# A transformer-like layer on one core: the merge projection opens with two jobs in seven products, first loads go out on ScalarE's queue, and the planner's rule for waiting changes

## The chip, the cores and the metric

The kernel runs on one core of one Trainium2 chip. The metric is the device time of one execution in microseconds (us), as the median of the runs. The core has five engines that run side by side and wait for each other through semaphores: TensorE (PE, matrix products into banks of PSUM), VectorE (DVE), ScalarE (ACT), GpSimd (POOL) and SyncE (SP, which here issues most of the DMAs). PEld is the loading of a matmul's stationary operand, which runs beside the matmuls.

## The reference: what is computed

One layer of a hybrid encoder over a sequence of 1024 positions with 1024 channels, in float32:

```python
h = rms_norm(x, norm1_w[l])
proj = h @ w_in[l]                    # q, k, v, gates, x_lru, y_lru: 8192 columns
...
y_a = (o * silu(g_ret)) @ w_ret_o[l]  # branch A: chunkwise retention, group norm
...
y_b = (hl * gelu(y_lru)) @ w_lru_o[l] # branch B: conv, gated linear recurrence
mix = (sigmoid(gate_ret + merge_gate_b[l, 0]) * y_a
       + sigmoid(gate_lru + merge_gate_b[l, 1]) * y_b)
x = x + mix @ w_out[l]                # the merge projection
h = rms_norm(x, norm2_w[l])
up = h @ ffn_w_up[l]                  # 6144 columns
...
x = x + (gelu(gate) * val) @ ffn_w_down[l]
return rms_norm(x, norm_f_w)
```

## The kernel before

**Matrix products.** Every large product is cut into jobs. A job multiplies a stationary block A of 256 rows or columns by 1024 with an operand B of 1024 by 1024. A is cut in 2 x 2 blocks (A11, A12, A21, A22; the second digit is the half of the inner dimension), B in 2 x 2 sets (B11 to B22), each set four tiles of 128 x 512 (j = 0 to 3). Float32 precision comes from a split: each tile is written as hi + lo, with hi a cast on ScalarE (L469) and lo a subtraction on DVE (L470). One product of a block with a set is then 4 tiles x 3 passes (`PASSES`, L399: hi hi, hi lo, lo hi) = 12 matmuls of 128 x 128 by 128 x 512 into one bank.

There are two ways through a job. The plain one, `mm_by` (L660, its matmuls at L680), takes eight products. The fast one, `mm_fast` (L698, matmuls at L718), takes seven, by the scheme of Strassen and Winograd. It needs sums of A's blocks (S1 to S4, formed on DVE in `prep_fast`, L545, at L555 to L564) and sums of B's sets (T1 to T4), and more additions behind the products: ScalarE copies a bank away at L767, and DVE adds at L735 to L771. The order of the seven products is a tuple (L400 to L405): `PRODS`, `ENDING`, `EARLY`, and `FIRST = ("A11", "S3", "A12", "S1", "S2", "A22", "S4")`, which no job uses. When S3 comes before S2 (`back3`, L703), two more DVE additions run, at L769 and L771. A job with `mate=True` is taken together with the next one: each product is done for both before the following one, so that a set of B is read twice in a row. Banks are six (`psg`, L439), tiles for A's blocks 22 (`NW`), all other tiles 81 (`NU`).

**Merge projection.** The four jobs `wjobs` (L1746) compute x + mix @ w_out, 256 positions each. A comes from `mix_d` in DRAM, where the last projection of branch B (`emit_lru_o`, L1396) writes the mixed channels; blocks with inner half 1 can be read when the first four channel groups of 128 are there, those with inner half 2 when all are. B is w_out: `w_out_set` (L1736) loads its sets, and their sums T1 to T4 were formed earlier and lie in `tw_d`. `out_start` (L1742) queues the building of B: the four plain sets first, then the four sums. Job 0 is plain, with inner half 1 ahead of half 2 (`by="k"`), and gives the set B12 back after it (`drop12`); jobs 1 to 3 are fast, one at a time, in the order `PRODS`. `emit_out` (L1667) adds x where the fast path has not (L1673), stores the row block and squares it on ScalarE for the norm that follows.

**What sets the order.** The program is built twice. The first build gives the list of instructions and their dependencies to the class `Plan` (L200). `latest` (L261) goes backwards and finds for each instruction when it is due; `forward` (L307) then lays out every engine in time with the durations of its cost model and takes the instruction with the earliest due time (`rank`) among those that are ready. This holds for the DMAs of SP's queue too, which are held back to what the model lets the DMA engines move. The second build is chained into these orders. At L341 to L346 DVE and ScalarE may be left idle for an instruction that is not ready yet: when it becomes ready within the next one's duration plus `NEAR` (500 ns), is overdue already, and the next one can spare more than `APART` (10,000 ns).

**Start.** The layer begins with the value projection (`values`, L1411). POOL issues the first eight columns of the parameters (L1478), ScalarE's queue the first x tile (L1479), and SP's queue weights and the other x tiles in turn (L1480 to L1491). Twelve matmuls on zeros (L1484) warm TensorE up. The first scaled x tile (L1439, on DVE) needs the parameters and the x tile, and the first matmul (L1454) needs that.

**End.** The last half tile is finished in two pieces by `final_half` (L1886): a sum of squares (L1892), its addition (L1893), a product with the norm's weights (L1894), then the root on POOL (L1897), two scalings (L1902, L1904) and two stores (L1905).

Of the kernel before, what the change touches and what calls it, by code (L numbers as in the profile page):

```python
# [199 lines left out]
class Plan:  # L200
# [5 lines left out]
    READ, WRITE, MOVE, QUEUE = 1900.0, 1500.0, 700.0 / 262144, 500.0  # L206
    LATE_DMA, LATE_PE, BACKLOG, KEEP = 1500.0, 400.0, 300.0, 2000.0
    SURE_DMA = 700.0
    NEAR, APART = 500.0, 10000.0

    @staticmethod
    def read(nc):
# [94 lines left out]
    def forward(self, rank):  # L307

        todo = {n: len(b) for n, b in self.before.items()}
        at = dict.fromkeys(self.steps, 0.0)  # L310
        free = dict.fromkeys(self.ENGINES, 0.0)
        wait = {e: [] for e in self.ENGINES}
        ready = {e: [] for e in self.ENGINES}
        order = {e: [] for e in self.ENGINES}
        moved, table, begin = 0.0, None, []
        for n, k in todo.items():
            if not k:
                heapq.heappush(wait[self.steps[n].eng], (0.0, n))

        def switch(n):  # L320
            f = self.steps[n].func
            return f in self.TABLES and table not in self.TABLES[f]

        left = len(self.steps)
        while left:
            t, e = math.inf, None
            for k in self.ENGINES:
                if not ready[k] and not wait[k]:
                    continue
                when = free[k] if ready[k] else max(free[k], wait[k][0][0])  # L330
                if k == "SP":
                    when = max(when, moved - self.READ - self.BACKLOG)
                if when < t:
                    t, e = when, k
            while wait[e] and wait[e][0][0] <= t:
                n = heapq.heappop(wait[e])[1]
                heapq.heappush(ready[e], (rank[n], n))
            item = ready[e][0]
            if e == "Activation" and switch(item[1]) and item[0] > t + self.KEEP:
                item = min((q for q in ready[e] if not switch(q[1])), default=item)  # L340
            if e in ("DVE", "Activation"):  # L341
                soon = min(((rank[n], at) for at, n in wait[e] if at < t + self.steps[item[1]].hold + self.NEAR),
                           default=None)
                if soon and soon[0] < min(t, item[0] - self.APART):
                    free[e] = soon[1]
                    continue  # L346
            ready[e].remove(item)
            heapq.heapify(ready[e])
            n = item[1]
            s = self.steps[n]  # L350
            if e == "Activation" and switch(n):
                t += self.SWITCH
                table = self.TABLES[s.func][0]
            order[e].append(n)
            if e == "PE":
                begin.append(t)
            left -= 1
            free[e] = t + s.hold
            if s.dma:
                if e == "Pool":  # L360
                    moved += s.bytes * self.MOVE
                    done = t + s.hold + self.landing(s)
                elif s.bytes > 4096:
                    moved = max(t + s.hold + self.landing(s) - s.bytes * self.MOVE - self.QUEUE,
                                moved) + s.bytes * self.MOVE
                    done = moved + self.QUEUE
                else:
                    done = t + s.hold + self.landing(s)
            else:
                done = t + s.hold + s.tail  # L370
            for m in self.after[n]:
                lag = self.lag(s, self.steps[m])
                if lag is not None:
                    if s.dma:
                        lag = max(self.HAND + self.SURE_DMA, min(lag, rank[m] - done))
                    at[m] = max(at[m], done + lag)
                todo[m] -= 1
                if not todo[m]:
                    heapq.heappush(wait[self.steps[m].eng], (at[m], m))
        return order, begin  # L380
# [45 lines left out]
def tile_trunk_layer(ctx, tc, x, xt, positions, params, consts, normf, w_in, w_v, w_ro, w_lo,  # L426
                     w_out, w_up, w_dn, w_gate, out):
    nc = tc.nc
# [895 lines left out]
    def operand(op, fetch, sums=True, sets=("B11", "B12", "B21", "B22")):  # L1324

        keys = [(n, j) for n in sets for j in range(4)]
        for key, (tick, t) in zip(keys, reads(fetch, keys, AHEAD_B)):
            yield from landed(tick)
            op[key] = split(t)
            put(t, late=SOONER)  # L1330
            yield 0.6
        if sums:
            yield from tsets(op, fetch)

    def kept_sums(op, src):

        def fetch(n, j):
            t = get()
            SY.dma_start(t, src[int(n[1]) - 1, j])
            return t  # L1340

        keys = [(f"T{i}", j) for i in (1, 2, 3, 4) for j in range(4)]
        for key, (tick, t) in zip(keys, reads(fetch, keys, AHEAD_B)):
            yield from landed(tick)
            op[key] = split(t)
            put(t, late=SOONER)
            yield 0.6
# [63 lines left out]
    def values():  # L1411
# [10 lines left out]
        def wload(nm, j):  # L1422
            m, kh = int(nm[1]) - 1, int(nm[2]) - 1
            t = raw[nm, j] = vget()
            SY.dma_start(t, w_v[4 * kh + j, :, TH * m:TH * m + TH])

        def xload(nm, j, q=SY):
            kh, h = int(nm[1]) - 1, int(nm[2]) - 1
            t = xs[nm, j] = get()
            q.dma_start(t, xt[4 * kh + j, :, TH * h:TH * h + TH])  # L1430
# [44 lines left out]
                         t.rearrange("p (m c) -> p m c", m=2))  # L1475
            put(t)

        G.dma_start(par[:, 0:8], params[:, 0:8])  # L1478
        xload("B11", 0, nc.scalar)  # L1479
        wload("A11", 0)  # L1480
        S.activation(st[:, 0:1], st[:, 1:2], AF.Sqrt)
        warm = psa.get()
# [2 lines left out]
        psa.put(warm)  # L1485
        for j in (1, 2, 3):
            wload("A11", j)
            xload("B11", j)
        for j in range(4):
            wload("A12", j)  # L1490
            xload("B21", j)  # L1491
# [175 lines left out]
    def emit_out(t, fast):  # L1667
        def emit(m, c, src, unit):
            if fast and unit is not None:
                acc = unit  # L1670
            else:
                acc = wjobs[t].take(m, c)
                V.tensor_add(acc, src, acc)  # L1673
                if unit is not None:
                    put(unit)
            i = 2 * t + m
            ST.dma_start(x1_d[x_row(t, m, c)], acc)
            j = psa.get()
            S.activation(j, acc, AF.Square, accum_out=nst[:, c, i:i + 1])
            psa.put(j)  # L1680
            if t == 3:
                last4[m, c] = acc
            else:
                put(acc)
        return emit

    def out_post(t):
        def fn():
            a, b, v, r, w = (nst[:, i, 2 * t:2 * t + 2] for i in range(5))
            V.tensor_add(v, a, b)  # L1690
            V.tensor_scalar(v, v, 1.0 / D, EPS, ALU.mult, ALU.add)
            G.tensor_tensor(r, v, half[:, 0:2], ALU.pow)
            if t >= 2:
                return norm_half(t - 2)
        return fn
# [44 lines left out]
        return t  # L1740

    def out_start():  # L1742
        builders.append(operand(wop, w_out_set, False))
        builders.append(kept_sums(wop, tw_d))

    wjobs = [Job(lambda m, kh, t=t: mix_d[t, m, kh].rearrange("p k c -> p (k c)"), wop,  # L1746
                 emit_out(t, t > 0), out_post(t), fast=t > 0, last=t == 3, drop12=t == 0,
                 pre=((0, 0), (0, 1), (1, 1)), fetch=from_x(t), by=None if t else "k",
                 order=None if t else ("A11", "A21", "A12", "A22"),
                 ready=lambda m, kh, t=t: all((4 * kh + j, t // 2) in mixed for j in range(4)))  # L1750
             for t in range(4)]
    ojobs[-2].post = out_start
# [86 lines left out]
    nf = []  # L1839
# [46 lines left out]
    def final_half(u, s):  # L1886

        one, two, r = nst[:, 0, 2:3], nst[:, 4, 0:1], nst[:, 3, 2:3]
        if s.start == 0:
            fin["o"], fin["j"] = get(), get()  # L1890
        o, j = fin["o"], fin["j"]
        V.scalar_tensor_tensor(j[:, s], u[:, s], 1.0 / D, u[:, s], ALU.mult, ALU.mult, accum_out=two)  # L1892
        V.tensor_add(one, one, two)  # L1893
        V.tensor_mul(o[:, s], u[:, s], nf[1][:, s])  # L1894
        if s.start == 0:
            return
        G.tensor_tensor(r, one, half[:, 0:1], ALU.pow)  # L1897
        put(u, j)
        for c in range(2):
            t = fin.pop((0, 0)) if c == 0 else o  # L1900
            if c:
                V.tensor_scalar(t, t, r, None, ALU.mult)  # L1902
            else:
                S.activation(t, t, AF.Copy, scale=r)  # L1904
            (SY if c else nc.scalar).dma_start(out[128 * 3:128 * 4, TH * c:TH * c + TH], t)  # L1905
            put(t)
# [104 lines left out]
```

## Time and profile before

| | |
|---|---|
| median of 3 runs | 1580.39 us (1579.16 to 1580.98) |
| the profiled execution | 1579.13 us |
| its span in the trace | 1577.3 us |
| TensorE busy | 1566.6 us (99%) |
| DVE busy | 1373.0 us (87%) |
| ScalarE busy | 933.9 us (59%) |
| DMA engines, mean | 179 GB/s |
| granted clock | 0.999 |

The profile is one execution, with times from the start of its span. A group line has line, engine, operation, out<-in by the program's names (g: banks of the products, w: tiles of A's blocks, u: other tiles, a: small banks), shape and count, then the busy time and the mean ns of one, then the engine's idle time ahead of it and what ended it. A timeline line has start and length in us, and in brackets the idle time before and its releaser. An engine with a q (SPq) is its queue, which issues DMAs.

### The profile page before, as it was taken

Reading aid. Unit: us, or ns where it says so; the run is one execution under the profiler, and the core shown is the slowest. Engines: PE = TensorE matmul, PEld = TensorE weight load, DVE = VectorE, ACT = ScalarE, POOL = GpSimd, SP = SyncE. Lnnn points to the kernel's source line nnn. Section 1 sums busy time; section 2 is a strip of 40 time slices with the busy share of each in tenths; the row PEclk is TensorE's granted clock in tenths of the full one; section 3 lists DMA queues with packets and bytes.
Section 4 is the critical chain, followed back from the end, with each engine's and each line's share of the span. In section 5 each row is a group of like instructions: output and inputs, shape, how many; then the busy total and the mean of one; then the engine's idle time right before and its main releaser. Section 6 shows DMA issues by size and latency. Waiting matters only on the chain.

```text
span 1577.3 us, 21478 instructions
## 1 busy us (share of the span) xinstructions
PE 1566.6 (99%) x7013; PEld 1294.2 (82%) x7013; DVE 1373.0 (87%) x2470; ACT 933.9 (59%) x1586; POOL 52.6 (3%) x74
## 2 busy tenths in 40 slices
PE   9999999999999999999999999999999999999998
PEld 7888888888888888888888888888888888888887
DVE  8999988898899888999997899777777778987885
ACT  7547964655567696955365764444444446563653
POOL 0001000000000000000000001000000000000000
PEclk9999999999999999999999999999999999999999
DMA  9344334444454245684996246444444456787752
GB/s 324 114 127 140 127 127 152 136 154 168 124 178 153 75 146 180 225 276 162 306 376 233 92 123 218 134 143 140 138 138 138 139 190 218 256 284 269 262 181 87
DMA packets 159328, 282.11 MB, mean 179 GB/s; under 512 B 17256, under 2 KB 29680, under 8 KB 159216
## 3 DMA queue, kind: packets, MB, share of 16 engines
q1 hardware_dynamic: 153664, 264.74, 51.1%
q0 software_dynamic: 4256, 13.64, 2.9%
q10 hardware_dynamic: 1296, 2.36, 0.4%
q8 instruction: 55, 0.90, 0.2%
q14 instruction: 57, 0.47, 0.1%
HBM read 195.73 MB, written 83.89 MB: 177 GB/s over the span
## 4 chain that ended last, share of the span: by engine, by line
PE 90%; DVE 4%; ACT 3%; DMA 1%; issue 1%; POOLq 0%; ACTq 0%; DVEq 0%; SPq 0%
PE g L718 78%; PE g L1454 5%; PE a L1130 2%; PE g L680 1%; DVE w L470 1%; PE a L1239 1%; PE a L1241 1%; PE a L1250 1%; PE a L1233 0%; PE a L1300 0%; DMA u<-td_d 0%; PE a L1720 0%; ACT u L469 0%; DMA u<-w_dn 0%; DMA w<-mix_d 0%
## 5 line engine op out<-in xcount | busy, mean ns | idle before, releaser
L718 PE MATMUL g<-u,w 128*128 128x512 f32 x5976 | 1390.1, 391 | 1.6 <-ACT u L767 1.5
L718 PEld LDWEIGHTS g<-u,w 128*128 128x128 f32 x5976 | 1115.2, 188 | 231.9 <-ACT u L767 3.5
L469 ACT CAST w<-w 128x512 fp32r<-128x512 f32 x516 | 316.6, 621 | 355.3 <-PE g L718 254.8
L470 DVE TENSOR_TENSOR w<-w,w 128x512 fp32r<-128x512 f32 x516 | 349.1, 682 | 63.3 <-ACT w L469 57.7
L747 DVE TENSOR_TENSOR u<-g,u 128x512 f32<-128x512 f32 x213 | 145.4, 684 | 52.9 <-PE g L718 43.7
L469 ACT CAST u<-u 128x512 fp32r<-128x512 f32 x233 | 138.4, 620 | 56.9 <-PE g L718 5.4
L767 ACT COPY u<-g 128x512 f32<-128x512 f32 x215 | 124.9, 582 | 61.6 <-PE g L718 59.4
L470 DVE TENSOR_TENSOR u<-u,u 128x512 fp32r<-128x512 f32 x233 | 152.8, 681 | 3.3 <-ACT u L469 2.8
L1769 DVE SCALAR_TENSOR_TENSOR u<-u,par,u 128x511 f32<-128x511 f32 x96 | 71.2, 743 | 2.9 <-ACT u L1766 2.6
L1454 PE MATMUL g<-w,u 128*128 128x512 f32 x264 | 61.9, 390 | 1.2 <-DVE u L1439 1.0
L1454 PEld LDWEIGHTS g<-w,u 128*128 128x128 f32 x264 | 49.3, 188 | 12.3 <-issue 1.5
L1774 POOL DMA_DIRECT2D ff_d<-u x48 | 36.1, 752 | 451.5 <-DVE u L1773 451.5
L1130 PE MATMUL a<-u,u 128*128 128x512 f32 x192 | 50.7, 393 | 0.3 <-ACT u L469 0.2
L555 DVE TENSOR_TENSOR w<-w,w 128x512 f32<-128x512 f32 x71 | 48.4, 682 | 1.4 <-DMA w<-w_lo 0.7
L558 DVE TENSOR_TENSOR w<-w,w 128x512 f32<-128x512 f32 x71 | 48.5, 684 | 0.9
L561 DVE TENSOR_TENSOR w<-w,w 128x512 f32<-128x512 f32 x71 | 48.4, 682 | 0.3
L564 DVE TENSOR_TENSOR w<-w,w 128x512 f32<-128x512 f32 x71 | 48.4, 682 | 0.3
L1766 ACT ACTIVATE u<-u,par 128x512 f32<-128x512 f32 x48 | 39.2, 816 | 16.0 <-DVE u L747 15.9
L741 DVE TENSOR_TENSOR u<-u,u 128x512 f32<-128x512 f32 x45 | 30.9, 686 | 16.9 <-ACT u L767 16.6
L1130 PEld LDWEIGHTS a<-u,u 128*128 128x128 f32 x192 | 35.5, 188 | 9.3 <-ACT u L469 1.3
L1773 DVE TENSOR_TENSOR u<-u,u 128x512 f32<-128x512 f32 x48 | 32.8, 686 | 6.1 <-ACT u L1772 6.1
L1112 DVE SCALAR_TENSOR_TENSOR u<-u,par,u 128x511 f32<-128x511 f32 (+2 forms) x48 | 35.7, 743 | 2.4 <-ACT u L1108 2.2
(211 smaller groups left out, 1130.4 us busy)
## 6 DMA issues: line engine op xcount, KB each, us to landing
w<-w_in SPq DMA_DIRECT2D x96, 256.0 KB, 2.7
w<-w_up SPq DMA_DIRECT2D x96, 256.0 KB, 2.7
u<-w_dn SPq DMA_DIRECT2D x84, 256.0 KB, 3.8
u<-x_d SPq DMA_DIRECT2D x60, 256.0 KB, 4.3
x_d<-u SPq DMA_DIRECT2D x48, 256.0 KB, 3.6
ff_d<-u POOLq DMA_DIRECT2D x48, 256.0 KB, 2.7
td_d<-u SPq DMA_DIRECT2D x48, 256.0 KB, 3.0
u<-td_d SPq DMA_DIRECT2D x48, 256.0 KB, 4.8
```

Of the source, the lines that this page charges most:

```text
L469: S.copy(hi, src)
L470: V.tensor_sub(lo, src, hi.bitcast(F32))
L555: V.tensor_add(s, r["A21"], r["A22"])
L558: V.tensor_sub(s, s, r["A11"])
L561: V.tensor_sub(s, r["A12"], s)
L564: V.tensor_sub(src, r["A21"], r["A11"])
L718: PE.matmul(bank[:, s], w[a][:, c], need(op, (SETS[nm], j))[b][:, s], start=first and n == 0, stop=n == 11, skip_group_check=True)
L747: V.tensor_add(u, bank, u)
L767: S.copy(u, bank)
L1130: PE.matmul(ps, wg[g][a][:, cs], xs[k][b], start=q == 0, stop=q == 5)
L1454: PE.matmul(bank, o[p][:, c], w[q], start=first and j == n == 0, stop=j == 3 and n == 2, skip_group_check=True)
L1769: V.scalar_tensor_tensor(c[:, s:], src[:, :TH - s], w, c[:, s:], ALU.mult, ALU.add)
```

## The change

- The planner's rule for waiting: `NEAR` and `APART` go. An instruction is now waited for when it becomes ready within the next one's duration (with the 1283 ns of a table switch, where that one needs it on ScalarE), is due before that duration and `MARGIN` (600 ns) are over, and the next one is due later than the awaited one's end by `EXTRA` (2000 ns).
- The first eight columns of the parameters go out on ScalarE's queue, ahead of the first x tile, and the second x tile behind it; POOL and SP lose one issue each.
- All four merge jobs are fast. Jobs 0 and 1 are a pair in the order `FIRST`; B's parts are built in the order B11, T3, B21, T1, T2, T4, B22, by `kept_or` (L1351), which loads a plain set from w_out and a sum from `tw_d`. B12 is not built.
- In `final_half` the addition of the sum of squares is ordered ahead of the product with the norm's weights.

```diff
-    NEAR, APART = 500.0, 10000.0
+    MARGIN, EXTRA = 600.0, 2000.0
...
             if e in ("DVE", "Activation"):
-                soon = min(((rank[n], at) for at, n in wait[e] if at < t + self.steps[item[1]].hold + self.NEAR),
-                           default=None)
-                if soon and soon[0] < min(t, item[0] - self.APART):
+                cost = self.steps[item[1]].hold
+                if e == "Activation" and switch(item[1]):
+                    cost += self.SWITCH
+                soon = min(((rank[n], at, self.steps[n].hold) for at, n in wait[e] if at < t + cost), default=None)
+                if soon and soon[0] < t + cost + self.MARGIN and item[0] > soon[1] + soon[2] + self.EXTRA:
                     free[e] = soon[1]
                     continue
...
-        G.dma_start(par[:, 0:8], params[:, 0:8])
+        nc.scalar.dma_start(par[:, 0:8], params[:, 0:8])
         xload("B11", 0, nc.scalar)
+        xload("B11", 1, nc.scalar)
         wload("A11", 0)
...
         for j in (1, 2, 3):
             wload("A11", j)
-            xload("B11", j)
+            if j > 1:
+                xload("B11", j)
...
     def out_start():
-        builders.append(operand(wop, w_out_set, False))
-        builders.append(kept_sums(wop, tw_d))
+        builders.append(operand(wop, kept_or(w_out_set, tw_d), False, ("B11", "T3", "B21", "T1", "T2", "T4", "B22")))
 
     wjobs = [Job(lambda m, kh, t=t: mix_d[t, m, kh].rearrange("p k c -> p (k c)"), wop,
-                 emit_out(t, t > 0), out_post(t), fast=t > 0, last=t == 3, drop12=t == 0,
-                 pre=((0, 0), (0, 1), (1, 1)), fetch=from_x(t), by=None if t else "k",
-                 order=None if t else ("A11", "A21", "A12", "A22"),
+                 emit_out(t, True), out_post(t), fast=True, last=t == 3,
+                 pre=((0, 0), (0, 1), (1, 1)), fetch=from_x(t), mate=t == 0, prods=FIRST if t < 2 else PRODS,
...
         V.scalar_tensor_tensor(j[:, s], u[:, s], 1.0 / D, u[:, s], ALU.mult, ALU.mult, accum_out=two)
-        V.tensor_add(one, one, two)
-        V.tensor_mul(o[:, s], u[:, s], nf[1][:, s])
+        a = V.tensor_add(one, one, two)
+        b = V.tensor_mul(o[:, s], u[:, s], nf[1][:, s])
         if s.start == 0:
             return
+        tc.add_manual_dep(b.ins, a.ins.name, mybir.DependencyInfo(mybir.DependencyClass.NoSync,
+                          mybir.DependencyReason.DATA), reason="the sum first")
```

## Prediction

> **What bounds the kernel now.** I read the page first, then the waits of TensorE, then its timeline around the merge projection, at the start and at the end. The page says that there is little else than matmuls to shorten:
>
> ```profile
> span 1577.3 us, 21478 instructions
> ...
> PE 1566.6 (99%) x7013; PEld 1294.2 (82%) x7013; DVE 1373.0 (87%) x2470; ACT 933.9 (59%) x1586; POOL 52.6 (3%) x74
> ...
> PE 90%; DVE 4%; ACT 3%; DMA 1%; issue 1%; POOLq 0%; ACTq 0%; DVEq 0%; SPq 0%
> ```
>
> TensorE (PE) is busy for 99% of the span and carries 90% of the chain that ended last; DVE comes second with 87%. So one matmul less is its own length less, as long as its inputs come in time. What TensorE waits for, in the whole run:
>
> ```profile
> PE g L718 <- ACT u L767: 1.5, 3, 0.8
> PE a L1484 <- DVE heat L1648: 1.3, 1, 1.3
> PE g L1454 <- DVE u L1439: 1.0, 1, 1.0
> PE a L1130 <- ACT u L469: 0.2, 1, 0.2
> ```
>
> These are 4.0 us in six waits. One lies at the start (L1439, 1.0 us), and three (1.5 us together) are products that wait for ScalarE to copy a bank away (L767). Two of those three stand right where the change works:
>
> ```profile
> 788.15 3.03 PE L718 MATMUL g<-u,w 128*128 128x512 f32 x12 [0.52 <-ACT u L767]
> 791.02 1.98 PE L680 MATMUL g<-u,w 128*128 128x512 f32 x8
> 793.77 5.74 PE L718 MATMUL g<-u,w 128*128 128x512 f32 x24 [0.78 <-ACT u L767]
> 799.35 9.23 PE L680 MATMUL g<-u,w 128*128 128x512 f32 x40
> 808.42 2.66 PE L718 MATMUL g<-u,w 128*128 128x512 f32 x11
> 810.91 11.06 PE L680 MATMUL g<-u,w 128*128 128x512 f32 x48
> 821.81 37.79 PE L718 MATMUL g<-u,w 128*128 128x512 f32 x166
> ```
>
> L680 is the first merge job in eight plain products, 8 + 40 + 48 = 96 matmuls, and L718 is every job in seven products. The first 48 of L680 need only the first half of the mixed channels. They are laid between the last products of the job before, and so fill the time until the second half has come back from DRAM. At 810.91 the other 48 start without a gap. The merge itself is dense; the engines around it are less so:
>
> ```profile
> 780.00:790.00 10.00, 9.48 (x42) 7.55 (x41) 8.11 (x14) 5.22 (x10) 0.00 (x0) 1.00 1.08 380
> 790.00:800.00 10.00, 9.22 (x41) 7.31 (x40) 9.56 (x16) 6.04 (x11) 0.00 (x0) 1.00 1.06 374
> 800.00:810.00 10.00, 10.00 (x45) 8.26 (x44) 8.16 (x13) 5.00 (x9) 0.00 (x0) 1.00 1.07 393
> 810.00:820.00 10.00, 10.00 (x46) 8.26 (x44) 9.35 (x16) 8.39 (x16) 0.00 (x0) 1.00 1.05 385
> 820.00:830.00 10.00, 10.00 (x46) 8.28 (x45) 8.63 (x16) 4.16 (x10) 0.72 (x1) 1.00 1.03 354
> 830.00:840.00 10.00, 10.00 (x46) 8.29 (x45) 8.68 (x15) 6.66 (x14) 0.00 (x0) 1.00 0.98 354
> 840.00:850.00 10.00, 10.00 (x46) 8.29 (x45) 9.80 (x22) 3.82 (x9) 1.07 (x1) 1.00 0.67 214
> 850.00:860.00 10.00, 10.00 (x48) 8.31 (x47) 6.05 (x10) 5.42 (x12) 0.00 (x0) 1.00 0.51 177
> ```
>
> The columns are the length, then busy time of PE, weight loads, DVE, ACT and POOL, the clock, the DMA share and GB/s. The DMA engines are full from 780 to 830 (share 1.03 to 1.08). DVE idles 1.89 + 0.44 + 1.84 + 0.65 + 1.37 + 1.32 + 0.20 = 7.71 us from 780 to 850 and 3.95 us in the ten after.
>
> **The opening pair.** Jobs 0 and 1 are taken together, product by product, in the order FIRST, both in seven products. Before, they took eight and seven. So one product of 12 matmuls goes. The 166 matmuls from 821.81 took 37.79 us, 0.228 each: **12 x 0.228 = 2.73 us less on TensorE**. The filler stays: A11 and S3 of both jobs are again 4 x 12 = 48 matmuls that need only the first half of the channels. What it costs elsewhere goes by these rows:
>
> ```profile
> L469 ACT CAST w<-w 128x512 fp32r<-128x512 f32 x516 | 316.6, 621 | 355.3 <-PE g L718 254.8
> L470 DVE TENSOR_TENSOR w<-w,w 128x512 fp32r<-128x512 f32 x516 | 349.1, 682 | 63.3 <-ACT w L469 57.7
> L747 DVE TENSOR_TENSOR u<-g,u 128x512 f32<-128x512 f32 x213 | 145.4, 684 | 52.9 <-PE g L718 43.7
> L767 ACT COPY u<-g 128x512 f32<-128x512 f32 x215 | 124.9, 582 | 61.6 <-PE g L718 59.4
> ```
>
> - Job 0 plain: 4 splits of its blocks (one ACT cast and one DVE subtraction each) and one DVE addition for each of four outputs, 8 on DVE. Job 0 in seven: 7 splits, 4 block sums, and 9 for the outputs (three added inputs at L741, three bank sums at L747, two at L769 and L771 because S3 comes before S2, one at L1673): 20. That is 12 more.
> - Job 1 was in seven already; the order FIRST adds its two at L769 and L771: 2 more.
> - The set B12 is no longer needed: 4 loads, 4 casts and 4 subtractions less.
> - Sum on DVE: 12 + 2 - 4 = 10 instructions of 0.684 = **6.84 us more**. ACT: 3 - 4 casts of 0.621 and 3 copies of 0.582 = 1.13 us more. DMA: 4 loads of 256 KB less, in a stretch that is full.
>
> The pair can also hold six banks, X, Y and Z of both jobs, which is all that the products have; no row shows that state, and the longest wait for a bank now is 0.8 us (L767), which I count with the rule for waiting.
>
> The cover for DVE is its idle time of 7.71 us until 850, but TensorE now needs the stretch 2.73 us sooner, so 4.98 remain. The other 1.86 us have to be pushed behind the pair, where the window from 850 has 3.95 idle. Against this, the whole run has no TensorE wait on L470 in its list, so the blocks and sets are ahead of their use. I cost the extra DVE work at nothing on the path. If none of the idle time can be used it is 6.84 us late, which is the rival below.
>
> **Start.** The first matmul of the layer waits for the first eight columns of the parameters:
>
> ```profile
> 0.74 0.41 ACTq L1430 DMA_DIRECT2D u<-xt  x1
> ...
> 1.25 4.06 PE L1484 MATMUL a<-heat 128*128 128x512 bf16 x12 [1.25 <-DVE heat L1648]
> 1.27 0.70 POOL L1478 DMA_DIRECT2D par<-params  x1 [0.82 <-POOLq L1996]
> ...
> 4.23 0.62 ACT L469 CAST w<-w 128x512 fp32r<-128x512 f32 x1 [1.55 <-DMA w<-w_v]
> ...
> 5.71 0.49 DVE L1439 TENSOR_SCALAR u<-u,par 128x512 fp32r<-128x512 f32 x1 [4.52 <-DMA par<-params]
> ...
> 6.35 2.03 PE L1454 MATMUL g<-w,u 128*128 128x512 f32 x6 [1.03 <-DVE u L1439]
> ```
>
> ```profile
> u<-xt SPq DMA_DIRECT2D x15, 256.0 KB, 5.4
> ...
> u<-xt ACTq DMA_DIRECT2D x1, 256.0 KB, 3.7
> ...
> par<-params POOLq DMA_DIRECT2D x1, 4.0 KB, 4.4
> ```
>
> POOL issued them at 1.27, they took 4.4 us, and DVE started at 5.71. ScalarE's queue starts at 0.74. With the parameters first in it, the x tile is issued 0.41 later, at 1.15. With the 3.7 us of the same tile in the trace it lands at 4.85, and is then the last to come. DVE starts at 4.9 in place of 5.71: **0.8 us less**. What is late next is the warm-up, which holds TensorE until 1.25 + 4.06 = 5.31, so no more than 6.35 - 5.31 = 1.04 can be gained. At the other end, if the tile took the 5.4 us of its kind on SP's queue, it would land at 6.55 and the start be 0.9 us later than now. I take 0.8, since the row with 3.7 is this very load, in an empty queue. The second x tile is third in ScalarE's queue, at about 1.6, where SP issued it at 1.66, and all loads behind it on SP move up by one issue. Behind the two added issues (0.82 us) on ScalarE stand a table load and, at 4.23, a cast that had waited 1.55 us for its load; that wait hides them.
>
> The Trainium skill, "DMA: Bandwidth & Descriptors", section "Issuing engines are not separate DMA queues", says that transfers of all issuing engines share the same 16 engines, and that issuing from several saves no more than issue time. No row here has two x tiles on ScalarE's queue; the rule speaks against a start that is sooner by more than an issue, and is taken up as a rival.
>
> **End.** In the last half tile the sum of squares waited behind a product that is needed later:
>
> ```profile
> 1571.83 0.08 DVE L1892 DVE_READ_ACCUMULATOR u<-u 128x1 f32 x1
> 1571.83 0.42 DVE L1894 TENSOR_TENSOR u<-u,u 128x256 f32<-128x256 f32 x1
> 1572.17 0.15 DVE L1893 TENSOR_TENSOR nst<-nst 128x1 f32<-128x1 f32 x1
> 1572.46 0.54 POOL L1897 TENSOR_TENSOR nst<-nst,half 128x1 f32<-128x1 f32 x1 [1.93 <-DVE nst L1893]
> 1573.04 0.48 DVE L1902 TENSOR_SCALAR u<-u,nst 128x512 f32<-128x512 f32 x1 [0.72 <-POOL nst L1897]
> ```
>
> With the sum first, L1893 starts when the accumulator is read, at 1571.91 and not at 1572.17: **0.26 us less**. The bounds are 0 and the 0.42 of L1894. L1894 then ends at about 1572.5, before L1902 needs it.
>
> **The rule for waiting.** The planner now leaves DVE or ACT idle when an operation that is due becomes ready within the next one's length and that next one can spare over 2 us. What is queued behind is that postponed operation and all after it on the engine, late by at most its length: 0.68 on DVE, 0.62 on ACT, more with a table switch. For: the 1.5 us of waits on L767 are of this kind, an urgent copy behind something else. But here that was a cast on a load that came later than planned, and a changed order does not make the load come sooner. Bounds: 1.5 us gained; in loss, three unhidden DVE waits, 2.0 us. I take 0, where nothing has a row.
>
> **Sum.** 2.73 + 0.8 + 0.26 = 3.8 us. The profiled execution took 1579.13 us (span 1577.3 and 1.83 around it), so 1575.3. The median of the runs before is 1580.39, 1.26 above the profiled one: **1576.6 us**. About 0.2% (3.2 us) is what a measurement of this kernel can tell from no change.
>
> **Rivals.**
> - *More goes: 1574.8.* The start gains its full 1.04, and the 1.5 us of waits on L767 go with the new order: 5.5 us. For it: both are waits in the list. Against it: the late loads. 15%.
> - *The start gains an issue only: 1577.0.* Loads share what the DMA engines move, the x tile lands as late as the parameters did but for the one issue of 0.41 that SP is relieved of: 2.73 + 0.41 + 0.26 = 3.4 us. For it: 5.4 us on SP's queue. Against: 3.7 on ScalarE's. 10%.
> - *The product saved becomes a wait: 1578.0.* Loads for the pair go out as A11, A21, A22, A12, two of each, so both A22 may precede the A12 that is due first. At 385 GB/s a tile of 262 KB takes 0.68 us, so A12 lands 1.36 later while the filler is no longer: 3.8 - 1.4 = 2.4 us. For: 810.91 starts without slack to spare in a full DMA stretch. Against: the planner orders SP by due times, and four loads have gone. 18%.
> - *Slower, DVE bounds the opening: 1586.2 at the worst.* The place is the pair. Its blocks must be summed, split and added up in 38 us, and DVE's idle time there is what casts lost waiting for loads, so it may be no use. The net change is 6.84 - u - 1.06 when u is the part that idle time and postponement take up. Slower than before below u = 5.8, slower by 0.2% below u = 2.6; with u = 0 it is 5.8 us slower. For: 4.98 us of idle time in which 6.84 must go. Against: no wait on L470, and 3.95 us of room right after. 17%, two thirds of it over 0.2%.
> - *The rule for waiting costs more than it gives: 1580.4.* DVE is at 9.80 of 10 in one window above; six unhidden waits of 0.68 are 4.1 us and eat the gain. 5%.
>
> The forecast has the remaining 35%. **Chances:** the forecast and the first two rivals, of which the second lies at the bound, 0.55 for faster; 0.32 within; 0.13 slower. **Range:** 1574.2 to 1582.0. It leaves out a tenth below, most of the first rival's end, and the worst of the DVE rival.
>
> **What would show it.** In the profile after: no L680; L718 with 84 more matmuls, 6060; the first L1454 at about 5.5 with a wait under 0.4; L1893 ahead of L1894. Right on the pair: no new PE wait on L470 or L469 between 790 and 850. Wrong: such waits (DVE rival), a gap ahead of A12's matmuls ended by a cast on w<-mix_d (load rival), or new waits on L767 elsewhere (rule for waiting).

## The result and the profile after

The changed kernel takes **1577.95 us** (median of 20 runs, 1576.32 to 1579.73), the one before 1580.21 on the same chips (20 runs, 1578.81 to 1582.2). The ratio is 0.9986, with an interval of [0.998, 0.9992]: 2.3 us less, between 1.3 and 3.2. That is faster, as forecast, but by 0.6 of the 3.8 us that were forecast.

The profiled execution took 1578.12 us. Its page has these lines in place of the ones shown of before:

```profile
span 1576.3 us, 21457 instructions
...
PE 1563.9 (99%) x7001; PEld 1292.0 (82%) x7001; DVE 1379.3 (88%) x2480; ACT 931.6 (59%) x1583; POOL 51.3 (3%) x73
```

TensorE has the 12 matmuls less that were counted (7013 to 7001) and 2.7 us less busy time; DVE has the 10 instructions more. But the span of this one execution is only 1.0 shorter. The list of TensorE's waits in the whole run (total, times, longest) says what became of the rest:

```profile
PE g L720 <- ACT u L769: 2.5, 4, 1.2
PE a L1487 <- DVE heat L1652: 1.3, 1, 1.3
PE g L1456 <- DVE u L1441: 0.8, 1, 0.8
PE a L1724 <- ACT a L1683: 0.5, 1, 0.5
PE g L720 <- ACT w L471: 0.3, 1, 0.3
PE g L720 <- ACT u L471: 0.3, 1, 0.3
```

Line numbers are two to four higher than before: L720 was L718, L769 was L767, L471 was L469, L1724 was L1720. The list was 4.0 us and is 5.7. The start's wait has gone from 1.0 to 0.8 only, waits for ScalarE's copies of banks have grown from 1.5 to 2.5, and there are three new ones, all on ScalarE.

**The opening** of the merge projection, TensorE's timeline:

```profile
792.21 15.26 PE L720 MATMUL g<-u,w 128*128 128x512 f32 x66 [0.84 <-ACT u L769]
807.76 24.50 PE L720 MATMUL g<-u,w 128*128 128x512 f32 x106 [0.29 <-ACT w L471]
```

L680 is gone. A copy is waited for as before, and where the second half of the mixed channels is first needed stands a wait of 0.29 for a cast (L471). The timeline of DVE and ScalarE just ahead of it tells which block it is:

```profile
806.36 1.41 DVE L557 TENSOR_TENSOR w<-w,w 128x512 f32<-128x512 f32 x2 [0.29 <-DMA w<-mix_d]
807.08 1.75 ACT L471 CAST w<-w 128x512 fp32r<-128x512 f32 x3 [0.70 <-DVE w L557]
```

L557 (L555 before) is the sum S1 = A21 + A22. It waited for a load, the cast waited for it, and TensorE for the cast. So the product that TensorE takes up here is S1, not A12: the planner has loaded A22 first and put S1's first matmuls ahead of A12's.

What stood in this place before is the line at 808.42 in the prediction: 11 matmuls of L718 behind the 40 of L680. By the order in which the program takes its products they are of job 1, its A11, and they too need only the first half of the channels. So the filler was 59 matmuls, 48 of L680 and these 11, and the pair has 48. Before, the block that TensorE needed next was cast until 810.62, 0.3 us ahead of its use at 810.91:

```profile
810.00 0.62 ACT L469 CAST w<-w 128x512 fp32r<-128x512 f32 x1 [1.35 <-DMA w<-mix_d]
```

The 11 matmuls are 11 x 0.228 = 2.5 us of cover that the pair no longer has. The windows over the same stretch (length, PE, weight loads, DVE, ACT, POOL, clock, DMA share, GB/s) show where DVE's added work went:

```profile
780.00:790.00 10.00, 10.00 (x46) 8.29 (x45) 9.56 (x17) 5.45 (x10) 0.00 (x0) 1.00 1.08 385
790.00:800.00 10.00, 9.16 (x41) 7.26 (x40) 9.96 (x18) 7.17 (x14) 0.00 (x0) 1.00 1.06 382
800.00:810.00 10.00, 9.71 (x42) 7.50 (x42) 9.69 (x17) 7.36 (x15) 0.00 (x0) 1.00 1.06 376
810.00:820.00 10.00, 10.00 (x46) 8.26 (x45) 10.00 (x18) 6.92 (x14) 0.00 (x0) 1.00 0.97 343
820.00:830.00 10.00, 10.00 (x46) 8.29 (x45) 10.00 (x17) 2.49 (x5) 0.00 (x0) 1.00 0.88 275
830.00:840.00 10.00, 10.00 (x45) 8.28 (x45) 9.20 (x17) 7.44 (x17) 0.00 (x0) 1.00 1.01 361
840.00:850.00 10.00, 10.00 (x45) 8.26 (x44) 9.15 (x20) 3.92 (x9) 1.39 (x2) 1.00 0.64 232
```

DVE idles 0.44 + 0.04 + 0.31 + 0 + 0 + 0.80 + 0.85 = 2.44 us here, where it idled 7.71. So 5.27 of the 6.84 us added lie in what was idle time, and TensorE waits for no subtraction (L472) in this stretch. This is pair and rule together: in the kernel with the pair alone, below, DVE is busy for 65.04 us from 780 to 850, against 62.28 before, so 2.8 us more.

**The start**, from its timeline:

```profile
0.74 0.41 ACTq L1432 DMA_DIRECT2D u<-xt  x1
...
1.18 0.45 ACTq L1480 DMA_DIRECT2D par<-params  x1
...
1.66 0.45 ACTq L1432 DMA_DIRECT2D u<-xt  x1
...
5.99 0.48 DVE L1441 TENSOR_SCALAR u<-u,par 128x512 fp32r<-128x512 f32 x1 [4.80 <-DMA par<-params]
...
6.62 3.65 PE L1456 MATMUL g<-w,u 128*128 128x512 f32 x13 [0.84 <-DVE u L1441]
```

The parameters are second in ScalarE's queue, not first: the planner gave the x tile and the parameters one due time and put the later-written one ahead. Issued at 1.18, they release DVE at 5.99, where before they did at 5.71. The first matmul is at 6.62 in place of 6.35, and was forecast at 5.5.

**The end**, DVE and POOL:

```profile
1570.71 0.08 DVE L1894 DVE_READ_ACCUMULATOR u<-u 128x1 f32 x1
1570.83 0.16 DVE L1895 TENSOR_TENSOR nst<-nst 128x1 f32<-128x1 f32 x1
1570.91 0.42 DVE L1896 TENSOR_TENSOR u<-u,u 128x256 f32<-128x256 f32 x1
1571.14 0.59 POOL L1901 TENSOR_TENSOR nst<-nst,half 128x1 f32<-128x1 f32 x1 [1.72 <-DVE nst L1895]
```

The sum is ahead of the product. It starts 0.12 after the accumulator is read (1570.71 to 1570.83), where it started 0.34 after (1571.83 to 1572.17): 0.22 us, where 0.26 was forecast.

### The profile page after: what moved, and what is told of

The parts are those of the page before. It is cut to its first block, busy times and chain, and to the rows that moved or that the text cites. A ratio compares the mean times of both kernels' runs of the same rounds, so it can differ in the third digit from the quotient of the medians.

```text
span 1576.3 us, 21457 instructions
## 1 busy us (share of the span) xinstructions
PE 1563.9 (99%) x7001; PEld 1292.0 (82%) x7001; DVE 1379.3 (88%) x2480; ACT 931.6 (59%) x1583; POOL 51.3 (3%) x73
## 4 chain that ended last, share of the span: by engine, by line
PE 89%; DVE 5%; DMA 4%; ACT 1%; issue 1%; SPq 0%; POOLq 0%; ACTq 0%; DVEq 0%
PE g L720 78%; PE g L1456 4%; PE a L1132 3%; DMA w<-mix_d 1%; DVE w L472 1%; PE a L1241 1%; DVE u L472 1%; PE a L1243 1%; PE a L1252 1%; DMA u<-u_d 1%; DMA mix_d<-u 1%; PE a L1235 0%; DVE u L749 0%; PE a L1302 0%; DMA u<-td_d 0%
## 5 line engine op out<-in xcount | busy, mean ns | idle before, releaser
L720 PE MATMUL g<-u,w 128*128 128x512 f32 x6060 | 1408.9, 391 | 3.1 <-ACT u L769 2.5
L720 PEld LDWEIGHTS g<-u,w 128*128 128x128 f32 x6060 | 1130.6, 188 | 236.3 <-ACT u L769 4.1
L471 ACT CAST w<-w 128x512 fp32r<-128x512 f32 x519 | 318.4, 621 | 353.6 <-PE g L720 239.6
L472 DVE TENSOR_TENSOR w<-w,w 128x512 fp32r<-128x512 f32 x519 | 351.4, 682 | 54.7 <-ACT w L471 48.7
L471 ACT CAST u<-u 128x512 fp32r<-128x512 f32 x229 | 136.0, 620 | 59.0 <-DVE u L1583 5.2
L769 ACT COPY u<-g 128x512 f32<-128x512 f32 x218 | 126.8, 583 | 73.1 <-PE g L720 69.6
L472 DVE TENSOR_TENSOR u<-u,u 128x512 fp32r<-128x512 f32 x229 | 149.8, 681 | 3.5 <-ACT u L471 3.1
L1771 DVE SCALAR_TENSOR_TENSOR u<-u,par,u 128x511 f32<-128x511 f32 (+1 forms) x96 | 71.2, 743 | 2.9 <-ACT u L1768 2.6
L557 DVE TENSOR_TENSOR w<-w,w 128x512 f32<-128x512 f32 x72 | 49.1, 682 | 7.0 <-DMA w<-ff_d 3.0
```

The lines of the kernel that those rows point to most:

```text
L471: S.copy(hi, src)
L472: V.tensor_sub(lo, src, hi.bitcast(F32))
L557: V.tensor_add(s, r["A21"], r["A22"])
L720: PE.matmul(bank[:, s], w[a][:, c], need(op, (SETS[nm], j))[b][:, s], start=first and n == 0, stop=n == 11, skip_group_check=True)
L769: S.copy(u, bank)
L1771: V.scalar_tensor_tensor(c[:, s:], src[:, :TH - s], w, c[:, s:], ALU.mult, ALU.add)
```

## The experiments

Each kernel has 11 runs, the one with both pair and rule at the end five; each is compared with the kernel before on its own chip, and that kernel's medians there were 1579.6 to 1579.7 us. Single executions of one kernel scatter by 1.5 us and more either way, so times below are differences of medians and profiles serve for the place alone.

### One part at a time

My theory here was the prediction's sum, corrected for the start; the rival, that the rule for waiting had moved the time. Three kernels add one part to the kernel before; the fourth is the changed kernel with the old start. The first has this edit, the next two the parts of the diff shown above for the merge jobs and the planner:

```diff
-        G.dma_start(par[:, 0:8], params[:, 0:8])
+        nc.scalar.dma_start(par[:, 0:8], params[:, 0:8])
         xload("B11", 0, nc.scalar)
+        xload("B11", 1, nc.scalar)
...
-            xload("B11", j)
+            if j > 1:
+                xload("B11", j)
```

> The kernel before with the start of the change alone (parameters and second x tile on ScalarE's queue). In the profile of the changed kernel the parameters went out second, behind the first x tile, and landed at 5.89 us. Theory: this alone is slower, by 0.3 us at the first matmul (6.62 in place of 6.35) and up to 0.75 by 50 us; time 0.3 to 0.8 us above before. Rival, the prediction's step: 0.8 us faster, and what the changed kernel showed came of other parts.

> The kernel before with the opening pair alone. Theory: 2.73 us less TensorE work at the merge projection, of which about 1 us is given back at the turn from the second to the third stage near 1345, where TensorE comes sooner but loads in a full DMA stretch do not; time 1.4 to 2.2 us below before. Rival: DVE or late loads bound the opening, time within 1 us of before or above it. Second rival: nothing is given back, 2.7 us below.

> The kernel before with the new rule for waiting alone. In the changed kernel TensorE gained about 0.65 us between 140 and 205 and 0.8 between 580 and 650, and lost 0.5 at 710, against before. Theory: these come of the rule, time 0.5 to 1.2 us below before. Rival, the prediction's value: no difference, within 0.3 us.

> The changed kernel with the start of before. Theory: faster than the changed kernel by what its start costs, 0.3 to 0.8 us, so 2.5 to 3 us below before; first matmul at 6.35 again. Rival: slower than the changed kernel by 0.8 us, 1.4 us below before.

| kernel | median us | less the kernel before | ratio and interval |
|---|---|---|---|
| start alone | 1580.55 | +0.9 | 1.0005 [0.9996, 1.0014] |
| pair alone | 1579.38 | -0.3 | 0.9997 [0.9988, 1.0006] |
| rule alone | 1577.46 | -2.2 | 0.9987 [0.9978, 0.9996] |
| all but the start | 1577.03 | -2.65 | 0.9984 [0.9975, 0.9993] |

The parts that carried the forecast's sum, the pair and the start, bring nothing that can be measured, and the part priced at nothing brings what the whole change brings. Of the four theories only the last was met (2.5 to 3 us below before). The pair gave less than its theory, as the first rival had it, and the rule more than its theory or its rival. With the rule and without the start the pair is worth as little as alone: 1577.46 - 1577.03 = 0.4 us, the end included. The start alone is not shown to be slower (its interval holds 1), but it is not 0.8 us faster: that would be 0.9995, below the interval.

### The start: order in the queue

Was it the place in the queue? This kernel has the changed one's start with the two lines in the other order, so that the parameters are really first:

```diff
-        nc.scalar.dma_start(par[:, 0:8], params[:, 0:8])
         xload("B11", 0, nc.scalar)
+        nc.scalar.dma_start(par[:, 0:8], params[:, 0:8])
         xload("B11", 1, nc.scalar)
```

> The changed kernel with the parameters really first in ScalarE's queue: the two issues are swapped in the program, since the planner breaks the tie of equal due times in favour of the later one. Theory (the order in the queue is what failed): the parameters land by 3.5 us, the x tile is last at 4.9 to 5.5, first matmul at 5.5 to 6.0, 0.6 to 1.1 us sooner than in the changed kernel; time 2.8 to 3.4 us below before. Rival (128 pieces of 32 bytes are slow wherever they stand, each waiting its turn behind 2 KB pieces of the other queue): first matmul not before 6.3, time as the changed kernel.

It took 1578.08 us, 0.9991 [0.9982, 0.9999], no better than the changed kernel. Its timeline:

```profile
0.74 0.41 ACTq L1481 DMA_DIRECT2D par<-params  x1
...
1.18 0.93 ACTq L1432 DMA_DIRECT2D u<-xt  x2
...
5.96 0.49 DVE L1441 TENSOR_SCALAR u<-u,par 128x512 fp32r<-128x512 f32 x1 [0.91 <-DMA u<-xt]
...
6.59 2.77 PE L1456 MATMUL g<-w,u 128*128 128x512 f32 x11 [0.39 <-DVE u L1441]
```

Now the x tile releases DVE, at 5.96: the parameters came early and the tile late. Its two tiles on this queue took 5.7 us from issue to landing (median of the two), and the changed kernel's 5.5, where the one tile before took 3.7. So the theory of the order falls. The rival had the time right but not the reason, since the parameters were early here: whichever is put first, the other one is late, as if the loads shared what they get, and the first matmul stays at 6.6. All 14 traces say the same: the first matmul starts at 5.99 to 6.71 us in the eight kernels with the old start, 6.36 on average, and at 6.58 to 6.83 in the six with a new one, 6.68 on average. That is 0.3 us later, not 0.8 sooner.

### What gives the pair's gain back

TensorE's waits at the opening and behind it are where the pair's kernels differ from the others. Around 857 the transposes of the next norm wait for a small bank. Timeline of the changed kernel there:

```profile
855.45 0.68 DVE L1677 TENSOR_TENSOR u<-g,u 128x512 f32<-128x512 f32 x1
...
856.22 0.60 ACT L1683 ACTIVATE a<-u 128x512 f32<-128x512 f32 x1 [1.08 <-DVE u L1677]
...
857.00 0.66 PE L1724 MATMUL a<-cst,u 128*128 128x128 f32 x4 [0.48 <-ACT a L1683]
```

The last addition of an output (L1677) is late on the full DVE. ScalarE's square of it (L1683) has its elementwise result, which nobody reads, in a small bank. It ran 1.08 us later than ScalarE could have, and held the bank that the transposes (L1724) need. Three edits to the changed kernel test the three places where waits stood:

```diff
-            j = psa.get()
+            j = get()
             S.activation(j, acc, AF.Square, accum_out=nst[:, c, i:i + 1])
-            psa.put(j)
+            put(j)
```

> The changed kernel; in the merge projection the squares' unused result goes to an SBUF tile in place of one of the two small banks that the transposes of the next norm need too. Theory (the wait of 0.5 us at 856, and with it part of what the pair lost between 842 and 915, is that bank, held until late squares are done): no wait of a transpose on L1683, TensorE 0.5 to 1 us further ahead by 915; time 0.5 us less than the changed kernel. Rival: the transposes wait for something else at the same place, no change.

```diff
-                 mate=t == 0, prods=FIRST if t < 2 else PRODS,
+                 mate=t == 0, prods=FIRST if t < 2 else PRODS,
+                 order=("A11", "A21", "A12", "A22") if t < 2 else None,
```

(with the loads of A22 ordered behind job 0's A12 on SP's queue)

> The changed kernel with the two loads of A12 of the opening pair ahead of the two of A22 on SP's queue. In the changed kernel A22's loads went out first (802.43 and 802.79, A12's at 803.27), and A12's landed at 807.67, 1.3 us after the first. Theory: the gap ahead of A12's matmuls (0.29 us and smaller ones behind it, 0.5 in all) goes, 0.3 to 0.5 us less. Rival: A22's sums come late in turn and TensorE waits there, no change.

```diff
-            if i == NF - 2:
+            if i == NF - 3:
```

(which starts the loads of the projection down one block earlier)

> The changed kernel with the building of the first down-projection operand offered one job earlier. In the changed kernel 1.04 us of the lead over before was lost near 1345, where a bank copy on ScalarE stood behind casts on loads of a full DMA stretch. Theory: loads that start earlier spread the stretch, the wait of 1.2 us on L769 goes, 1 us less than the changed kernel. Rival: free tiles, not the offer, set when these loads start, no change.

| kernel | median us | less the kernel before | ratio and interval |
|---|---|---|---|
| squares' result in SBUF | 1576.46 | -3.3 | 0.9981 [0.9972, 0.999] |
| A12 ahead of A22 | 1578.93 | -0.8 | 0.9995 [0.9986, 1.0004] |
| projection down's loads earlier | 1577.12 | -2.6 | 0.9982 [0.9973, 0.9991] |

With A12 first TensorE still waits at the opening: for a copy (1.5), for A12's subtraction (0.2) and, at 817.95, for a cast (0.7). By the order in which the program takes its products, that cast is of S1 of job 1, which needs A22. So the rival is borne out: A22's sums come late in turn.

```profile
PE g L724 <- ACT u L773: 1.8, 2, 1.5
...
PE g L724 <- ACT w L471: 0.7, 1, 0.7
...
PE g L724 <- DVE w L472: 0.2, 1, 0.2
```

In the kernel with the squares in SBUF the whole list of waits is short, and holds none on a small bank:

```profile
PE g L720 <- ACT u L769: 1.8, 3, 0.8
PE a L1487 <- DVE heat L1652: 1.3, 1, 1.3
PE g L1456 <- DVE u L1441: 0.3, 1, 0.3
```

The third edit was to remove a wait of 1.22 us at 1346 that the changed kernel's timeline has:

```profile
1346.36 5.98 PE L720 MATMUL g<-u,w 128*128 128x512 f32 x25 [1.22 <-ACT u L769]
```

In the edited kernel's timeline there is none:

```profile
1329.65 22.60 PE L720 MATMUL g<-u,w 128*128 128x512 f32 x99
```

But the pair alone and the kernel with A12 first have none there either, without this edit, so this wait does not come with the pair alone, and one trace does not show that the edit removed it. Neither interval, of the squares or of the earlier loads, is clear of the changed kernel's: at these two places the profile shows what became of the waits, and the time does not show what that is worth.

### Pair and rule, with the waits relieved

The last four kernels share three edits (the old start, squares in SBUF, loads of the projection down earlier) and the new end. They have both of pair and rule, one, or neither. If the waits above gave the pair's gain back, the pair must now bring its 2.7; if the rule had only hidden the pair's waits, it must now bring nothing.

> Pair and rule, with the two places relieved where the lead was given back: squares' unused result in SBUF, first down-projection operand offered a job earlier; start as before, end as in the changed kernel. Theory (the pair is worth its 2.73 us less about 0.7 of longer waits at its opening when nothing gives it back later): 4 to 5 us below before, the fastest kernel so far. Rival (what the pair saves is always lost at the next stage, whose DVE and ACT work sets its end): about 3 us below before.

> The same as the kernel with pair and rule and both places relieved, but with the merge projection of before. Theory: 2 us slower than that one, 2 to 3 us below before. Rival (the pair is worth nothing): the same time as that one.

> Pair and both places relieved, with the old rule for waiting. The pair alone gained 0.3 us, in a trace where the bank and load waits at its opening had grown from 1.3 to 3.1 us. Theory (rule and pair work on each other: the old rule leaves urgent copies behind casts that wait for loads): 2 us slower than pair and rule together, 1 to 2.5 us below before. Rival (their gains add up): the rule's own gain slower, 1.5 to 2 us below before with opening waits as small as with the rule.

> The kernel before with the two places relieved and the end of the changed kernel, neither pair nor rule. Theory: little alone, 0 to 1 us below before, since before lost less at these places (0.65 us of bank and copy waits at 900 and 0.3 at 1346) than the changed kernel did. Rival: the two relieved places are worth 1.5 us or more in any kernel, and are not tied to the change.

| kernel | median us | less the kernel before | ratio and interval |
|---|---|---|---|
| neither | 1578.92 | -0.7 | 0.9994 [0.9985, 1.0003] |
| rule | 1576.8 | -2.8 | 0.9981 [0.9972, 0.999] |
| pair | 1576.69 | -2.9 | 0.9977 [0.9968, 0.9985] |
| both | **1574.94** | **-4.7** | 0.9967 [0.9954, 0.9979] |

Here the pair is worth 1578.92 - 1576.69 = 2.2 us without the rule and 1576.8 - 1574.94 = 1.9 with it; the rule 2.1 and 1.75. They add up within the scatter, as the rival of the third expectation had it; its theory, that pair and rule work on each other, falls. Without the relief the pair was worth 0.3 and 0.4 (both tables above), so the relief makes the difference, some 1.7 us; its two edits are not told apart by the times. The pair alone on the kernel before (0.9997) and the pair here (0.9977) have intervals that don't meet; relief and new end without the pair are worth 0.7 of that. The kernel with both is the fastest of the study, and its interval lies clear of the changed kernel's, by a hair.

Two kernels with the old rule and the pair, in the groups by line and shape (busy, mean ns, idle before): the pair alone,

```profile
L718 PE MATMUL g<-u,w 128*128 128x512 f32 x6036 | 1406.8, 391 | 3.7 <-ACT u L767 2.5 <-ACT w L469 0.8 <-ACT u L469 0.2
...
L1720 PE MATMUL a<-cst,u 128*128 128x128 f32 x64 | 9.8, 272 | 0.5 <-ACT a L1679 0.5
```

and the pair with the waits relieved:

```profile
L718 PE MATMUL g<-u,w 128*128 128x512 f32 x6036 | 1406.2, 391 | 1.8 <-ACT u L767 1.1 <-ACT w L469 0.7
...
L1720 PE MATMUL a<-cst,u 128*128 128x128 f32 x64 | 10.3, 273 | 0.0
```

The kernel before has in the same groups:

```profile
L718 PE MATMUL g<-u,w 128*128 128x512 f32 x5952 | 1387.2, 391 | 1.6 <-ACT u L767 1.5
...
L680 PE MATMUL g<-u,w 128*128 128x512 f32 x96 | 22.3, 389 | 0.0
```

The pair alone saves 1387.2 + 22.3 - 1406.8 = 2.7 us of products, and pays 3.7 - 1.6 = 2.1 in waits ahead of them and 0.5 ahead of the transposes: 2.6. Relieved, it pays 1.8 - 1.6 = 0.2. These are two single executions. Of the 2.4 between them 1.0 lies behind the opening, where the squares' edit acts, and 1.3 in the opening, where no edit acts; there the planner's order is another in the relieved kernel, so that this 1.3 comes of the relief is not shown. TensorE's waits by stretch, added up from the lists of all 14 kernels, show which part of this comes back each time:

| | opening, 780 to 832 | 832 to 1000 | 1330 to 1360 |
|---|---|---|---|
| no pair: before, start, rule | 1.3, 2.2, 1.2 | 0, 0, 0 | 0.2, 0.4, 0.2 |
| no pair, relieved: rule, neither | 1.2, 1.5 | 0, 1.0 | 0, 0 |
| pair, squares in a bank: changed, pair, no start, parameters first, A12 first, earlier loads | 1.1, 3.1, 1.3, 0.8, 2.4, 1.5 | 1.1, 1.0, 1.4, 1.7, 0.6, 1.2 | 1.2, 0, 0.4, 0.9, 0, 0 |
| pair, squares in SBUF: that alone, both, pair relieved | 1.5, 2.4, 1.8 | 0, 0, 0 | 0, 0, 0 |

From 832 to 1000 the pair costs 0.6 to 1.7 us whenever the squares hold a bank, and nothing when they don't: this is shown, by six kernels against three. The wait of the transposes for the small bank itself is 0 to 1.1 of it; some 0.6 are waits for a copy and a cast near 900, which go with it, and why they do is not shown. The 1.0 of the relieved kernel with neither has another releaser, a DVE operation (L1712). The opening's waits are 1.5 on average without the pair (7.4 in five) and 1.8 with it (15.9 in nine), and spread widely: the 3.1 of the pair alone is one execution's, in a stretch where the DMA engines are full. But one kind of them is the pair's own. For casts and subtractions of A's blocks TensorE waits in eight of the nine kernels with the pair, 0.3 to 1.1 us (6.1 in nine, 0.7 on average), and in none of the five without it. With 0.7 off, 2.73 leaves 2.0, which is what the relieved pair measures (2.2 and 1.9).

## Why the prediction was right and wrong

Right were the direction and three pieces of the mechanism: the price of the twelve matmuls, the cover for DVE in the stretch watched, and the end. That the sum came as near as it did is luck. Pair and start were to bring 3.5 us and brought nothing that could be measured, and a term put at 0 brought 2.2.

Of the signs that the prediction set, L680 is gone, L718 has its 6060 matmuls, and the sum stands ahead of the product. The first matmul is at 6.62 and not at 5.5. A new wait on the cast of blocks (0.29, the old L469) stands in the opening, and waits for copies have grown elsewhere (1.2 at 1346). It had named the last as the sign of a costly rule; but the rule alone has 0.2 at 1346, as before, and is the part that gained.

| term | forecast us | measured us |
|---|---|---|
| pair | -2.73 | -0.3 alone (-1.9 to +0.9); -2.2 and -1.9 with the waits relieved |
| start | -0.8 | +0.9 alone (-0.6 to +2.2); +0.4 by medians in the changed kernel |
| end | -0.26 | -0.22 in the profile, too small to time |
| rule | 0 | -2.2 alone (-3.5 to -0.6); -2.1 and -1.75 with the waits relieved |
| sum | -3.8 | -2.3 (-3.2 to -1.3) |

**Pair.** The twelve matmuls went, at the price forecast. "I cost the extra DVE work at nothing on the path" is the step that failed, and not where I looked. In the stretch that I watched, 780 to 850, the cover held in the changed kernel: 5.27 us went into idle time, a little more than the 4.98 counted, and no product waited for a subtraction. But "the filler stays" was misread from the lines: the 11 matmuls at 808.42 were filler too, and it went from 59 matmuls to 48. That is 2.5 us less cover. Loads that went out sooner in the changed kernel (those of the second half from 802.43 on, before from 804.66) made up for most of it; the wait that is left is the 0.7 us on average found above. And I closed the account at the products. What DVE does last, the outputs' final additions, came later; ScalarE's squares came after them and held small banks, and TensorE met that at the next norm, 50 us behind the opening. I had looked at banks of products and at inputs, and not at who else takes small banks.

**Start.** "I take 0.8, since the row with 3.7 is this very load, in an empty queue" failed. The 3.7 us belonged to a load that had the queue for itself; with three loads in the queue the tiles took 5.5 and 5.7. The other bound, 0.9 later, was nearer. What the Trainium skill says in "DMA: Bandwidth & Descriptors", section "Issuing engines are not separate DMA queues", is borne out: by it the move could save issue time alone. It saved 0.09 us of it (the parameters were issued at 1.18 and not at 1.27), and the first matmul came no sooner. The forecast had also taken the program's order of the two lines for the queue's; the kernel with the order that I had meant shows that this alone decided nothing.

**Rule.** "I take 0, where nothing has a row" failed in size, beyond the far side of the range I had given (1.5 gained). The reason given against it holds for the waits in the list: those on the copies did not go (2.0 us in the kernel with the rule alone, 1.5 before). The gain is elsewhere. In the groups between 130 and 210 us, the kernel before and then the one with the rule alone:

```profile
L718 PE MATMUL g<-u,w 128*128 128x512 f32 x302 | 70.3, 390 | 0.1
L1130 PE MATMUL a<-u,u 128*128 128x512 f32 x48 | 12.5, 396 | 0.1
```

```profile
L720 PE MATMUL g<-u,w 128*128 128x512 f32 x305 | 70.9, 389 | 0.0
L1132 PE MATMUL a<-u,u 128*128 128x512 f32 x48 | 12.7, 392 | 0.0
```

Three matmuls more begin in the same 80 us, 0.7 us at 0.228 each, and the relieved pair of kernels, neither and rule, has 302 and 305 too. From 500 to 600 it is two matmuls (441 and 443) and in the relieved ones three (440 and 443), some 0.5 us. These are stalls too short for the list: the whole list had one of them, 0.2 on L1130. That makes 1.2 us located. The rule also loses: from 9 to 50 us two matmuls fewer begin (183 and 181, in the relieved kernels 182 and 180), 0.5 us. So 0.7 of 2.2 us are accounted for, and where the rest lies stays open. ScalarE loads five tables fewer (72 to 67, 1.28 us each), and the rule counts a switch; that the time comes from there is not shown.

**End.** Right: the sum went ahead, and 0.22 of the 0.26 us came.

**Rivals.** The product saved did become a wait in part. Loads of A22 went ahead of A12's, and TensorE took S1 first and waited for its cast; the price was 0.3 us in the changed kernel and 0.7 on average, not 1.36, and putting A12 first gained nothing. DVE as the bound of the opening did not happen. The start's rival was nearer than the forecast, yet still too good.

## What to carry to other kernels

Work taken off the busiest engine is worth its length only if what follows it, down to the last reader of the last output, can also come earlier: follow the added work of the other engines past the stage, and ask which buffer its last step holds and who needs that buffer next. Where work is to fill the time until a load lands, count all that stands there in the timeline, whatever job it is of. A load's time in the trace is that of its neighbours too: a row with one load in a queue is no price for three. A list of waits leaves out stalls of a few hundredths; when a change touches the order of many small operations, count the matmuls begun in a stretch of before and after.

## What the runs showed of the hardware

The same 4 KB of parameters, by the records of its packets in the trace: from POOL's queue they ran as 16 pieces of 256 bytes, from 4.26 to 5.31 us; from ScalarE's as 128 pieces of 32 bytes, from 3.78 to 5.53 among the other queue's pieces of 2 KB. Put first in that queue they ran from 2.12 to 3.34. So from ScalarE's queue, small rows were spread out over 1.2 to 1.75 us, against 1.05 from POOL's, and were through sooner only where they were first.
